# Larger GpSimd shares in the last rows and fewer load-to-load waits in a streaming row maximum

## The chip, the cores and the metric

One core of a Trainium2 chip. The time is device microseconds of one execution, the median of several. In the profile's lines DVE is VectorE, ACT ScalarE, POOL GpSimd and SPq the sequencer of SyncE, which issues the loads; L64 is line 64 of the kernel. Times are from the start of the span.

## The reference

```python
x = np.random.randn(8192, 8192).astype(np.float32)
return np.linalg.norm(x, ord=np.inf, axis=1)      # max |x| of each row
```

268 MB are read once and 32 KB written.

## The kernel before

Loads of two rows per partition (128 x 16384 floats, 8.39 MB) go through a ring of three places. VectorE reduces each with absolute maximum. In the last two loads and the pieces of the last row a share is left to ScalarE (absolute value in place) and GpSimd (maximum); a final reduce on VectorE takes the last piece and the partial results together.

```python
HEAD = 2
PAIRS = 30
TILES = (                                # (width, GpSimd's share of it)
    [[(8192, 0)]] * HEAD
    + [[(16384, 0)]] * (PAIRS - 1)
    + [[(16384, 7168)], [(8192, 3328)]]
    + [[(4160, 1760), (2080, 832), (1024, 384), (512, 0), (416, 0)]]
)
RING = 3 * 16384
...
            if final:
                buf = last[:, :w]
            else:
                if at + w > RING:
                    at = 0
                buf = ring[:, at : at + w]
                at += w
            nc.sync.dma_start(out=buf, in_=src[:, off : off + w])
...
            if final:
                pairs_out()
                absmax(res[:, R - 1 :], last)
```

The program's builder derives the waits. A load that takes over a place waits for the reduce that read it and also for the earlier load that filled it.

## Time and profile before

| | before |
|---|---|
| median of the first 6 runs | 628.58 us (628.52 to 628.62) |
| profiled span | 626.8 us |
| load queue busy | 99.1% of the span |
| between two loads | 19.35 us, of which VectorE works 17.22 |
| semaphore instructions at the load's line | 29 |
| start of the last two-row reduce to the end of the final reduce | 20.86 us |

Read the middle and the end apart. In the middle the stream of loads sets the pace. At the end, once the last two-row load has landed, what counts is who is ready last for the final reduce: the last landing, VectorE or GpSimd. The lines are in the prediction. One more, on the load's own line in the kernel before (engine, kind and count; then minimum, median and maximum in ns, and the first and last start in us):

```profile
L153 SPq EVENT_SEMAPHORE  x29: 17/17/27, 22.7 to 564.6; - x29
```

One extra semaphore instruction goes with each load that takes over a place: the wait for the earlier load, which half of the loads are to lose.

### The profile page before, as it was taken

The page shows a single profiled execution, that of the slowest core. Times are in us where ns is not written, and L with a number is a line of the kernel's source. Part 1 is how long each engine was busy: PE and PEld are TensorE (multiplying, and loading weights), DVE is VectorE, ACT ScalarE, POOL GpSimd, SP SyncE. Part 2 cuts the span into 40 slices and gives each one's busy share as a digit, 9 for nine tenths or more (in the row PEclk, how much of TensorE's full clock was granted, in tenths as well). Part 3 has the DMA queues.
Part 4 walks back from the last instruction along what each step waited for, and adds up shares of the span by engine and source line. Part 5 has one row for each costly group of instructions (what it writes and reads, how often), then busy time and mean ns, then how long its engine had stood idle before and what let it go on. Part 6 is the DMA issues. An engine that isn't in the chain of part 4 may idle for free.

```text
span 626.8 us, 218 instructions
## 1 busy us (share of the span) xinstructions
PE 8.7 (1%) x15; PEld 3.2 (1%) x15; DVE 537.5 (86%) x39; ACT 14.3 (2%) x10; POOL 13.3 (2%) x13
## 2 busy tenths in 40 slices
PE   0000000000000000000000000000000000000005
PEld 0000000000000000000000000000000000000002
DVE  1938988889988889888898888988889988889888
ACT  0000000000000000000000000000000000000034
POOL 0000000000000000000000000000000000000007
PEclk9999999999999999999999999999999999999999
DMA  8999999999999999999999999999999999999996
GB/s 368 435 468 402 468 402 468 402 468 402 468 402 468 402 460 410 452 418 448 422 448 422 418 452 402 468 402 468 402 468 402 468 402 468 402 468 402 460 402 278
DMA packets 5525, 268.47 MB, mean 428 GB/s; under 512 B 627, under 2 KB 789, under 8 KB 1045
## 3 DMA queue, kind: packets, MB, share of 16 engines
q1 hardware_dynamic: 5472, 268.44, 99.1%
q10 hardware_dynamic: 53, 0.03, 0.0%
HBM read 268.44 MB, written 0.03 MB: 428 GB/s over the span
## 4 chain that ended last, share of the span: by engine, by line
DMA 70%; DVE 29%; issue 0%; SPq 0%; PE 0%; ACT 0%; DVEq 0%
DMA ring<-in_x_dram 70%; DVE res L64 28%; DVE part L64 1%; DVE last L64 1%; SPq L153 0%; PE ps_ones L189 0%; ACT sb_ones L190 0%; DVEq L64 0%
## 5 line engine op out<-in xcount | busy, mean ns | idle before, releaser
L64 DVE TENSOR_REDUCE res<-ring 128x2 f32<-128x16384 f32 (+1 forms) x32 | 525.4, 16420 | 86.5 <-DMA ring<-in_x_dram 86.5
L82 ACT ACTIVATE ring<-ring 128x7168 f32<-128x7168 f32 (+4 forms) x5 | 12.2, 2449 | 577.0 <-DMA ring<-in_x_dram 577.0
L71 POOL TENSOR_REDUCE part<-ring 128x1 int32<-128x7168 int32 (+1 forms) x2 | 9.1, 4566 | 587.3 <-ACT ring L82 587.2
L108 PE MATMUL ps_warm<-ident 128*128 128x512 f32 (+1 forms) x12 | 8.2, 827 | 614.5 <-DVE part L64 613.2
L64 DVE TENSOR_REDUCE part<-ring 128x1 f32<-128x1024 f32 (+1 forms) x2 | 6.3, 3210 | 0.0
L108 PEld LDWEIGHTS ps_warm<-ident 128*128 128x128 f32 x12 | 2.9, 274 | 618.8 <-issue 615.3
L64 DVE TENSOR_REDUCE last<-ring 128x1 f32<-128x2400 f32 (+3 forms) x4 | 5.3, 1392 | 0.0
L71 POOL TENSOR_REDUCE last<-ring 128x1 int32<-128x1760 int32 (+2 forms) x3 | 3.0, 1017 | 0.4 <-ACT ring L82 0.4
L96 ACT ACT_TABLE_LOAD x1 | 1.3, 1283 | 31.5 <-DVE res L64 31.5
L64 DVE TENSOR_REDUCE res<-last 128x1 f32<-128x423 f32 x1 | 0.6, 594 | 0.1
L88 POOL MEMSET ident<- 128x128 f32 x1 | 0.2, 205 | 21.4 <-DVE res L64 21.4
L128 ACT COPY sb_pairs<-ps_pairs 30x128 f32<-30x128 f32 x2 | 0.4, 254 | 0.0
L71 POOL TENSOR_REDUCE res<-part 128x1 int32<-128x2 int32 x2 | 0.4, 196 | 0.1
L123 PE MATMUL ps_pairs<-ident,res 128*30 128x128 f32 x2 | 0.4, 272 | 0.0
L190 ACT COPY sb_ones<-ps_ones 4x128 f32<-4x128 f32 x1 | 0.3, 255 | 2.0 <-PE ps_ones L189 2.0
masks.py:199 POOL TENSOR_SCALAR_AFFINE_SELECT ident<-ident 128x128 f32<-128x128 f32 x1 | 0.3, 294 | 0.1
L189 PE MATMUL ps_ones<-ident,res 128*4 128x128 f32 x1 | 0.3, 272 | 1.3 <-DVE res L64 1.3
L123 PEld LDWEIGHTS ps_pairs<-ident,res 128*30 128x30 f32 x2 | 0.2, 106 | 0.6 <-POOL res L71 0.3
L96 ACT ACTIVATE ident<-ident 128x1 f32<-128x1 f32 x1 | 0.2, 203 | 0.0
L208 POOL MEMSET const-float32-0.0<- 128x1 f32 x1 | 0.1, 99 | 0.2 <-issue 0.2
L208 POOL MEMSET const-bfloat16-1.0<- 128x1 bf16 x1 | 0.1, 102 | 0.0
L208 POOL MEMSET const-uint8-127<- 128x1 uint8 x1 | 0.1, 102 | 0.0
(2 smaller groups left out, 0.2 us busy)
## 6 DMA issues: line engine op xcount, KB each, us to landing
ring<-in_x_dram SPq DMA_DIRECT2D x3, 4096.0 KB, 21.5
ring<-in_x_dram SPq DMA_DIRECT2D x1, 2080.0 KB, 35.7
ring<-in_x_dram SPq DMA_DIRECT2D x1, 1040.0 KB, 37.8
ring<-in_x_dram SPq DMA_DIRECT2D x1, 512.0 KB, 38.5
ring<-in_x_dram SPq DMA_DIRECT2D x30, 40.8
ring<-in_x_dram SPq DMA_DIRECT2D x1, 256.0 KB, 38.7
last<-in_x_dram SPq DMA_DIRECT2D x1, 208.0 KB, 38.7
out_dram<-sb_pairs ACTq DMA_DIRECT2D x1, 30.0 KB, 1.5
```

The source lines that it names most:

```text
L64: return keep(nc.vector.tensor_reduce(out=dst, in_=src, axis=X, op=MAX, apply_absolute_value=True,)).ins
L71: keep(pool.add_instruction(mybir.InstTensorReduce(name=nc.get_next_instruction_name(), ins=[pool.lower_ap(src.bitcast(INT32))], outs=[poo ...
L82: keep(nc.scalar.activation(src, src, mybir.ActivationFunctionType.Abs))
L88: nc.gpsimd.memset(ident, 0.0).ins, after.name,
L96: abs_ident = nc.scalar.activation(ident[:, :1], ident[:, :1], mybir.ActivationFunctionType.Abs)
L108: product = keep(nc.tensor.matmul(ps_warm[:, : w * P], lhsT=ident, rhs=ident.unsqueeze(1).to_broadcast([P, w, P]), start=True, stop=True,) ...
L123: keep(nc.tensor.transpose(ps_pairs[r], both[:, :, r], ident))
L128: keep(nc.scalar.copy(sb[:, :, r], ps_pairs[r]))
L189: nc.tensor.transpose(ps_ones, res[:, X_ONE:], ident)
L190: keep(nc.scalar.copy(sb_ones, ps_ones))
L208: nc = _bacc.Bacc("TRN2", target_bir_lowering=False, num_devices=1)
```

## The change

The intent: take work from VectorE at the end, where it is the last to be ready, and drop waits that a later wait contains.

```diff
-    + [[(16384, 7168)], [(8192, 3328)]]
-    + [[(4160, 1760), (2080, 832), (1024, 384), (512, 0), (416, 0)]]
+    + [[(16384, 7328)], [(8192, 3488)]]
+    + [[(4128, 1824), (2048, 864), (1024, 416), (512, 0), (480, 0)]]
...
-            nc.sync.dma_start(out=buf, in_=src[:, off : off + w])
+            load = nc.sync.dma_start(out=buf, in_=src[:, off : off + w]).ins
+            if not final:
+                if (len(loads) + 4) % 10 < 5:
+                    for a, v, earlier in loads:
+                        if a < at and at - w < a + v:
+                            tc.declare_no_dep(
+                                load, earlier, reason="ordered by the reduces in between",
+                            )
+                loads.append((at - w, w, load))
```

More of the change, by code (lines that the diff above doesn't have):

```diff
@@ L131, in pairs_out @@
         ))
+    loads = []
     at = 0
```

## The prediction

> **What bounds the kernel now.** I read the page from the top. Only two things are busy: VectorE, and the DMA engines.
>
> ```profile
> PE 8.7 (1%) x15; PEld 3.2 (1%) x15; DVE 537.5 (86%) x39; ACT 14.3 (2%) x10; POOL 13.3 (2%) x13
> ...
> DMA  8999999999999999999999999999999999999996
> ...
> q1 hardware_dynamic: 5472, 268.44, 99.1%
> ```
>
> The reader is to see that the load queue fills 99.1% of the span while VectorE, the busiest engine, has 86%. The next view is the chain that ended last, in order of time. It is periodic in the middle and of another kind at the end:
>
> ```profile
> 80.77 0.02 issue
> 80.80 17.23 DVE res L64
> 98.03 0.02 issue
> 98.04 40.78 DMA ring<-in_x_dram
> 138.83 0.02 issue
> ...
> 562.46 40.80 DMA ring<-in_x_dram
> 603.26 0.02 issue
> 603.28 8.69 DVE res L64
> 611.97 6.25 DVE part L64 x2
> 618.22 5.25 DVE last L64 x4
> 623.47 0.04 DVEq L64
> ```
>
> From 80.77 to 138.83 us three loads of two rows land: 58.06 / 3 = 19.35 us each. Each is 128 x 16384 x 4 bytes = 8.39 MB, so 433.5 GB/s. The reduce of such a load takes 17.22 us, so VectorE waits 2.13 us for every load. The chain passes through the reduce only because the ring has three places and load n is issued when the reduce of load n-3 ends. That does not make the reduce the limit: the load issued at 98.04 lands 40.78 us later, which is 2.13 us (rest of the load then moving) + 19.35 (the next) + 19.35 (itself) = 40.8. The queue still holds 21.4 us of work when a new load joins it.
>
> At 603.26 the last two-row load has landed and the character changes. From there VectorE has no gap: 8.69 + 6.25 + 5.25 us. The last timeline lines on VectorE, ScalarE and GpSimd give the race at the end:
>
> ```profile
> 613.04 2.98 ACT L82 ACTIVATE ring<-ring 128x3328 f32<-128x3328 f32 x1 [3.50 <-DMA ring<-in_x_dram]
> ...
> 618.14 5.32 DVE L64 TENSOR_REDUCE last<-ring 128x1 f32<-128x2400 f32 x4
> ...
> 619.71 3.08 POOL L71 TENSOR_REDUCE last<-ring 128x1 int32<-128x1760 int32 x3 [0.38 <-ACT ring L82]
> ...
> 623.55 0.59 DVE L64 TENSOR_REDUCE res<-last 128x1 f32<-128x423 f32 x1
> ```
>
> VectorE reaches 623.46, GpSimd 622.79; the last piece, issued at 584.09 with 38.7 us to landing, is there at 622.79. So the final reduce (623.55) waits for VectorE alone, by 0.67 us over both others. After it come 0.28 us of transpose, 0.26 us of copy and the store, all fixed.
>
> **What the Trainium skill says.** (1) "DMA: Bandwidth & Descriptors", section "Where 436 GB/s comes from", puts the ceiling of 16 ports at 435.2 GB/s. This trace has 433.5 in the middle: agreed, and no more than 0.4% can be gained there. (2) The same page, "Anatomy of one DMA": DMA engines do not wait on semaphores; a wait sits on the issuing sequencer before dispatch. The trace agrees: both waits of a load are SyncE's (29 and 29 times, next fence), and a removed wait can only help by an earlier issue. (3) The same page, "Two DMAs through the same engine are not ordered": the order a kernel has is the completion semaphore. The change keeps that order indirectly: the reduce has waited for the earlier load and the new load waits for that reduce. (4) "VectorE: DVE Perf Modes", "The perf-mode tier table": this reduce has only the 1x mode. At the 0.96 GHz that the page gives, one element a cycle is 1.042 ns; the trace's (17220 - 8686) / 8192 = 1.0417 ns agrees.
>
> **The change, part one: the waits.**
>
> ```profile
> SPq L153 <- DVE res L64: 490.9, 29, 17.2
> SPq L153 <- DMA ring<-in_x_dram: 77.7, 29, 20.1
> ```
>
> Each of the 29 loads that takes over a place has two waits. The first is an extra semaphore instruction at the load's line (x29, median 17 ns), which ends when the earlier load lands; the second ends 17.2 us later, when that load's reduce does. For example, SyncE issues at 78.69, waits 1.8 us for the landing at 80.77, then 17.2 us for the reduce until 98.03. The reduce cannot end before its own load has landed, so the DMA wait is always contained in the VectorE wait. Without it, the VectorE wait becomes about 19.0 us and ends at the same 98.03.
>
> Which loads: counting the ring's loads from 0, the condition picks numbers 6 to 10, 16 to 20 and 26 to 30, all of which take over a place, so 15 of the 29 (the one small piece that it also picks, number 36, has no wait instruction of its own now, as its predecessors have made that wait). I expect 14 semaphore instructions to remain at the load's line. Saved: 15 x 17 ns = 0.26 us of SyncE's time, spent while it waits anyway. On the issue of a load: 0. Even if each issue came 20 ns sooner, it would join a queue with 21.4 us in it. **Sum of part one: 0.00 us.**
>
> **Part two: the shares and the pieces.** VectorE's cost from its rows: 1.0417 ns an element plus a fixed 142 ns (1210 for 1024, 5209 for 4864, 675 for 512 all fit). ScalarE's absolute value: (6176 - 2977) / 3840 = 0.833 ns; GpSimd the same, (6164 - 2968) / 3840 = 0.832 ns.
> VectorE's elements, in order after the untouched 8192: 1024 becomes 864 (16384 - 8192 - 7328), 4864 becomes 4704, then 2400 to 2304, 1248 to 1184, 640 to 608, 512 stays, and the final 416 + 7 to 480 + 7. Before the final that is 160 + 160 + 96 + 64 + 32 = 512 elements fewer: 0.533 us. The final has 64 more: +0.067. If nothing else held it, the end would move by -0.467 us.
>
> Now what holds it. Landings: ScalarE starts on a piece some 0.10 us after it lands (603.36 against 603.26), so the one-row load landed at about 612.94. Today VectorE turns to it at 613.01; with 0.167 us less ahead of it, it would at 612.84, so it waits until about 612.96. Gain so far 0.05 instead of 0.167. After this: -0.217 at the next start (617.92; that piece, 32 elements shorter, lands at about 617.83), -0.317 (620.38; lands about 620.27), -0.384 (621.68; lands about 621.50), -0.417 for the 512 piece (622.36; lands about 622.22). The landing estimates are ScalarE's starts less 0.10, less the shift in the cumulated width (32 to 64 elements) at 19.35 us / 16384 = 1.18 ns. All are met with 0.1 us or so to spare. VectorE ends at 623.46 - 0.417 = 623.04. The last byte of the row is the same byte, so the final piece lands at 622.8 as now.
> GpSimd: its first long reduce starts 0.133 us later (609.74) and takes 6.30; the second, 3.10, starts at about 616.22 and ends at 619.32; after the small combine and ScalarE's 1824 (until 619.65) it runs 1.71 + 0.91 + 0.535 with gaps of 0.05, from 619.72 to about 622.97. That is 0.07 us before VectorE.
> So the final starts at about 623.13, takes 0.594 + 0.067 = 0.66, and ends at 623.79 instead of 624.14. **Sum of part two: -0.35 us. Both parts: 628.57 - 0.35 = 628.2 us**, which is 0.06%.
>
> **The rivals.** (a) GpSimd becomes the bound of the end. It is my nearest calculation, 0.07 us. For it: its chain will carry 13,920 elements instead of 13,472 and passes through ScalarE first. Against: today it has 0.67 us of slack. If each of its hand-overs from ScalarE costs 0.1 us more than I took, the end moves only -0.1 to -0.2: 628.4 us.
> (b) The waits cost the DMA stream something that these views don't show, such as a small gap between loads. For it: 433.5 stays 0.4% below the skill's ceiling, and 30 loads x 19.35 x 0.4% is 2.3 us; someone chose to drop exactly half of the waits. Against: the load is in the queue 21.4 us before its turn. If half of that came back, 627.1 us. I give this one chance in twenty.
> (c) The dropped wait comes back elsewhere: another semaphore wait in its place, for instance for the reuse of a semaphore. As it too would lie within the 17.2 us of the VectorE wait, it makes 628.2 as well, unless it waits for a load still moving: that would delay an issue by up to 19 us, of which the queue's 21.4 us covers all. So again nothing.
> (d) The gain at the end is lost because the last landing moves later: three pieces of the last row are a little smaller and begin at other addresses. The last five pieces land within 622.79 - 612.94 = 9.85 us against 9.68 at the steady rate, so all their overheads together are now 0.17 us. Even double that leaves the landing (622.96) before VectorE's 623.04. No change to the estimate.
>
> **Range and chances.** The executions before lie within 0.1 us (628.52 to 628.62). My uncertainties are rival (a), +0.2, the one-row landing, 0.1 either way, and the stream, which repeats to a few hundredths from load to load. The range is 627.85 to 628.6 us. A move of 2% would need 12.6 us. Nothing in the change can give that: the whole end after 603.26 is 23 us, and the stream is at the ceiling. Slower by 2% would need the queue to run dry, 21 us late on an issue. I put faster at 0.01, same at 0.98, slower at 0.01.
>
> **What would show it.** Right: 19.35 us between reduces in the middle and VectorE still waiting 2.13 us before each; 14 instead of 29 semaphore instructions at the load's line, with the waits for VectorE longer by about 1.8 us in those loads and the issues at the same times; in the end a short VectorE wait (up to 0.15 us) before the 4704 reduce, GpSimd's last reduce ending near 622.97, the final reduce of 487 elements starting near 623.13. Wrong: another period in the middle, or a gap in the queue (rival b); the final reduce starting well after VectorE's last one (rival a, or d if the landing is late). The whole would be wrong if the start of the stream moved, since every later time hangs on it.

## The result, and the profile after

The changed kernel took 628.28 us (628.14 to 628.70, 6 runs), the kernel before 628.58 us beside it. The ratio is 0.9996 with an interval of 0.9983 to 1.0009: the same, by the 2% rule. A ratio here is the mean time of one kernel's fast runs over that of the other's fast runs of the same rounds, so it is not quite the ratio of the medians quoted.

The profile alone would have misled. The profiled execution happened to be the slowest of the six, and its span is 626.9 us, 0.1 *longer* than before. First the end of its chain of waits:

```profile
582.27 31.14 DMA ring<-in_x_dram
613.41 0.03 issue
613.43 5.05 DVE part L64
618.49 5.05 DVE last L64 x4
623.54 0.04 DVEq L64
623.57 0.05 issue
623.62 0.67 DVE res L64
```

The chain before had VectorE work without a gap from 603.28 on. Now it comes off a landing at 613.41: VectorE was ready for the one-row load a little before it was there. The rest of the end is shorter: the last two-row reduce starts at 603.72, the final one ends at 623.62 + 0.66 = 624.28, which is 20.56 us against 20.86. So the end gained 0.30 us. The two others that the final reduce needs are GpSimd's last three reduces and the last piece, which was issued at 584.5:

```profile
620.13 3.04 POOL L71 TENSOR_REDUCE last<-ring 128x1 int32<-128x1824 int32 x3
last<-in_x_dram SPq DMA_DIRECT2D x1, 240.0 KB, 38.6
```

GpSimd was done at 623.17 and the piece landed at 623.1; VectorE was done at 623.5 and is still the last.

What hid it is in the middle, in VectorE's timeline of the same execution (start, duration, and in brackets the idle time before):

```profile
80.71 17.22 DVE L64 TENSOR_REDUCE res<-ring 128x2 f32<-128x16384 f32 x1 [2.13 <-DMA ring<-in_x_dram]
100.36 17.22 DVE L64 TENSOR_REDUCE res<-ring 128x2 f32<-128x16384 f32 x1 [2.43 <-DMA ring<-in_x_dram]
119.90 17.22 DVE L64 TENSOR_REDUCE res<-ring 128x2 f32<-128x16384 f32 x1 [2.32 <-DMA ring<-in_x_dram]
139.25 17.22 DVE L64 TENSOR_REDUCE res<-ring 128x2 f32<-128x16384 f32 x1 [2.14 <-DMA ring<-in_x_dram]
```

Two loads are 19.65 and 19.54 us apart instead of 19.35, another later is 19.41. Together that is 0.30 + 0.19 + 0.06 = 0.55 us lost. The first load landed 0.10 us earlier than before, so all that follows is 0.44 us later, and 0.44 - 0.30 is the longer span. Whether that slip belongs to the dropped waits is a question for the experiments.

Of the waits themselves, SyncE's view and the load's line:

```profile
SPq L155 <- DVE res L64: 518.2, 29, 19.3
SPq L155 <- DMA ring<-in_x_dram: 51.4, 14, 20.0
```

The semaphore instructions at the load's line, as above:

```profile
L155 SPq EVENT_SEMAPHORE  x14: 17/1719/1779, 22.6 to 565.0; - x14
```

Fifteen of the 29 waits for a landing are gone. The waits for VectorE, still 29, took 518.2 us instead of 490.9: 27.3 more, or 1.8 for each of the fifteen. The time saved in one wait came back in the next. The first load without its wait was issued at 78.60, before at 78.69: 0.09 earlier, as the whole stream is there (80.71 and 80.80 in the timelines). So dropping the wait did not move the issue. The median length of the semaphore instructions that stay is 1719 ns instead of 17; in both kernels SyncE waits some 1.8 us for such a landing, and why the instruction is recorded longer here isn't known.

### The profile page after: what moved, and what is told of

It reads as the page before. It is cut to its first block, busy times and chain, and to the rows that moved or that the text cites. A ratio compares the mean times of both kernels' runs of the same rounds, so it can differ in the third digit from the quotient of the medians.

```text
span 626.9 us, 203 instructions
## 1 busy us (share of the span) xinstructions
PE 8.8 (1%) x15; PEld 3.3 (1%) x15; DVE 537.1 (86%) x39; ACT 14.7 (2%) x10; POOL 13.5 (2%) x13
## 4 chain that ended last, share of the span: by engine, by line
DMA 70%; DVE 29%; SPq 0%; issue 0%; PE 0%; ACT 0%; DVEq 0%
DMA ring<-in_x_dram 70%; DVE res L64 28%; DVE part L64 1%; DVE last L64 1%; SPq L155 0%; PE ps_ones L201 0%; ACT sb_ones L202 0%; DVEq L64 0%
## 5 line engine op out<-in xcount | busy, mean ns | idle before, releaser
L82 ACT ACTIVATE ring<-ring 128x7328 f32<-128x7328 f32 (+4 forms) x5 | 12.6, 2523 | 577.0 <-DMA ring<-in_x_dram 577.0
L71 POOL TENSOR_REDUCE part<-ring 128x1 int32<-128x7328 int32 (+1 forms) x2 | 9.4, 4697 | 587.9 <-ACT ring L82 587.9
L64 DVE TENSOR_REDUCE part<-ring 128x1 f32<-128x864 f32 (+1 forms) x2 | 6.1, 3048 | 0.1
L64 DVE TENSOR_REDUCE last<-ring 128x1 f32<-128x2304 f32 (+3 forms) x4 | 5.1, 1342 | 0.0
L71 POOL TENSOR_REDUCE last<-ring 128x1 int32<-128x1824 int32 (+2 forms) x3 | 3.0, 1050 | 0.1
L88 POOL MEMSET ident<- 128x128 f32 x1 | 0.2, 204 | 21.3 <-DVE res L64 21.3
## 6 DMA issues: line engine op xcount, KB each, us to landing
ring<-in_x_dram SPq DMA_DIRECT2D x1, 256.0 KB, 38.5
last<-in_x_dram SPq DMA_DIRECT2D x1, 240.0 KB, 38.6
```

Source lines behind the costliest of these rows:

```text
L64: return keep(nc.vector.tensor_reduce(out=dst, in_=src, axis=X, op=MAX, apply_absolute_value=True,)).ins
L71: keep(pool.add_instruction(mybir.InstTensorReduce(name=nc.get_next_instruction_name(), ins=[pool.lower_ap(src.bitcast(INT32))], outs=[poo ...
L82: keep(nc.scalar.activation(src, src, mybir.ActivationFunctionType.Abs))
L88: nc.gpsimd.memset(ident, 0.0).ins, after.name,
```

## The experiments

My theory: the whole gain is at the end, because VectorE was last to be ready there; the dropped waits give nothing, as each lay within the wait for VectorE. Rivals: the dropped waits speed up the stream; they disturb it; GpSimd or the last landing is what binds the end. Times, and those of the kernel before on the same chip:

| run | what it is | median, us | before, us | end, us |
|---|---|---|---|---|
| e1 | new shares and pieces only | 628.39 | 628.81 | 20.56 |
| e2 | dropped waits only | 628.65 | 628.81 | 20.86 |
| e3 | the change, all waits dropped | 628.57 | 628.81 | 20.56 |
| e4 | the change again | 628.46 | 628.81 | 20.55 |
| e5 | still larger GpSimd shares | 628.87 | 628.77 | 21.06 |
| e6 | last pair as single rows | 628.79 | 628.77 | |
| e7 | ring of two places | 661.24 | 628.77 | |
| e8 | waits dropped in runs of fifteen, one run | 628.39 | 628.77 | 20.56 |
| e9 | single rows, fewer pieces | 628.69 | 628.56 | |
| e10 | the change a third time | 628.26 | 628.56 | 20.57 |

The last column is the yardstick: from the start of the last two-row reduce to the end of the final reduce. It is left out for e7 and where the end is built otherwise. e1 to e4 shared one set of runs of the kernel before (9). For e5 to e8 the record lists the same nine values and one more, so their "before" was mostly taken some minutes earlier; those runs are judged by their traces. e9 and e10 have a set of their own (9), on another chip. All results were correct.

### The two halves of the change alone (e1, e2)

e1 is the kernel before with the new `TILES`; e2 is the changed kernel with the old ones.

```diff
# e2, against the changed kernel
-    + [[(16384, 7328)], [(8192, 3488)]]
-    + [[(4128, 1824), (2048, 864), (1024, 416), (512, 0), (480, 0)]]
+    + [[(16384, 7168)], [(8192, 3328)]]
+    + [[(4160, 1760), (2080, 832), (1024, 384), (512, 0), (416, 0)]]
```

> Only the new shares and pieces, with all waits of the kernel before. Theory (the end is bound by VectorE, the waits do nothing): the whole gain, 628.25 us, 0.3 us under the kernel before, and the end relative to the start of the last two-row reduce as in the changed kernel (final reduce ends 20.57 us after it). Rival (the dropped waits give the gain): 628.55. Scatter of the executions: under 0.15 us if the dropped waits cause the scatter of the changed kernel (628.14 to 628.70), up to 0.5 us if it is chance.

> Only the dropped waits, with the shares and pieces of before. Theory: 628.57 us within 0.05, the loads 19.35 us apart, the final reduce ends 20.86 us after the start of the last two-row reduce, 14 semaphore instructions at the load. Rival (the waits cost the stream something): 628.3 or less, with loads closer than 19.35. Second rival (dropping them disturbs the stream): a median above 628.65 and a scatter of 0.5 us.

e1 took 628.39 us, 0.42 less than the kernel before beside it; e2 took 628.65, 0.16 less, with the kernel before scattering from 628.55 to 629.10. Taken alone, those times leave a little room for the rival. The end of e2's VectorE timeline decides more:

```profile
603.21 8.69 DVE L64 TENSOR_REDUCE res<-ring 128x1 f32<-128x8192 f32 x1 [2.14 <-DMA ring<-in_x_dram]
...
623.48 0.59 DVE L64 TENSOR_REDUCE res<-last 128x1 f32<-128x423 f32 x1
```

and of e1's:

```profile
603.54 8.69 DVE L64 TENSOR_REDUCE res<-ring 128x1 f32<-128x8192 f32 x1 [2.14 <-DMA ring<-in_x_dram]
...
623.44 0.66 DVE L64 TENSOR_REDUCE res<-last 128x1 f32<-128x487 f32 x1
```

The end is 20.86 us with the old pieces and 20.56 with the new, whatever the waits: e2 has the figure of the kernel before, e1 that of the changed one. In between, e2's two-row reduces start 19.34 to 19.36 us apart all along, as before. What is left of the 0.16 us is no more than the scatter, and e3 doesn't repeat it.

e1 also has a slip, with all its waits in place: two of its reduces start at 100.28 and 119.78, 19.50 us apart. So a slip needs no dropped wait.

### All waits dropped (e3), and in other runs (e8)

```diff
-                if (len(loads) + 4) % 10 < 5:
+                if True:                                # e3
+                if (len(loads) + 4) % 20 < 15:          # e8
```

> The changed kernel with the wait for the earlier load dropped from all loads instead of half. Theory: as the changed kernel, 628.25 us within 0.1; no semaphore instruction left at the load. If dropped waits help the stream, another 0.1 us or more under it; if they disturb it, twice the scatter and a higher median.

e3 took 628.57 us, 0.11 *more* than e4 with half of the waits dropped, which is within the scatter. If dropped waits helped, it should be the other way round. And one expectation was plainly wrong. The load's line in e3:

```profile
L155 SPq EVENT_SEMAPHORE  x25: 17/17/17, 98.3 to 562.8; - x25
```

Not 0 but 25 semaphore instructions are there: another wait took the place of the one removed. The page attributes all of SyncE's waiting at the loads to VectorE, none to a load, so these wait for something that has long happened. My reading: the loads use eight semaphores in turn, and before one is used again SyncE must know that its last load has landed. The first half can be checked: the kept traces name the semaphore that each load signals (the views do not print it), and in e3, e8 and the kernels before and after there are eight, in turn. Loads 8 to 32 are 25. In the change five loads without the wait follow five with it. Load n needs news of load n - 8. Each load that keeps its wait waits for the load three before it, so load n - 5 has brought that news. Then nothing comes back, which would explain why half of the waits were dropped and not all. e8 tests this reading by its count:

> Waits dropped in runs of fifteen loads instead of five. With all of them dropped 25 short semaphore instructions stood at the load again, the first ahead of load 8: I take it that the loads use eight semaphores in turn, and one is waited for before it is used again unless a later wait has told of it. Then this one has 7 waits of its own left and 13 to 15 come back (loads 8 to 10 and 21 to 30, perhaps two more), 20 to 22 in all. If nothing comes back: 7. The time is the same either way, 628.4.

```profile
L155 SPq EVENT_SEMAPHORE  x20: 17/17/1760, 98.5 to 564.7; - x20
```

20 it is: seven of its own and thirteen that came back. The time is 628.39 us in one run, the end 20.56 us. Rival (c) of the prediction, a wait that returns for the reuse of a semaphore, is real, though not in this change, and as harmless as it said.

### The change again (e4, e10)

> The changed kernel once more, to see whether the profiled slip of its stream (two loads 19.65 and 19.54 us apart instead of 19.35) comes at the same loads again. Theory (chance): 628.25 us, another profile without a slip or with one elsewhere. Rival (it belongs to the loads with dropped waits): the same two loads late by 0.3 and 0.2 us again, and a scatter of 0.5 us.

> The changed kernel beside it on the same chip, as the measure for a difference of 0.2 us, and a third profile of its stream. Theory: 628.45 us, loads 19.35 us apart with a slip at most by chance, the final reduce ends 20.57 us after the start of the last two-row reduce.

628.46 and 628.26 us, 0.35 and 0.30 below the kernel before beside them, after 0.30 in the first comparison. e10's two-row reduces start 19.34 to 19.36 us apart from first to last. e4 had one of 0.10 us at another load: 158.25 to 177.70 is 19.45. The slip is not at the same loads again, so nothing ties it to the loads without waits, and e1 has one without any dropped wait. All slips of 0.05 us or more in the kept traces (the changed kernel, e1, e3, e4 and e8) lie between 80 and 178 us; the other runs with three places have none. Whether they are more frequent with dropped waits was not tested: only the kernel before and e1 were profiled with all waits. What makes them isn't known.

### More for GpSimd (e5)

```diff
-    + [[(16384, 7328)], [(8192, 3488)]]
-    + [[(4128, 1824), (2048, 864), (1024, 416), (512, 0), (480, 0)]]
+    + [[(16384, 7648)], [(8192, 3808)]]
+    + [[(4128, 1984), (2048, 944), (1024, 464), (512, 0), (480, 0)]]
```

> The changed kernel with GpSimd's shares larger once more (7648, 3808, 1984, 944, 464). By my model of the end (landings, 1.0417 ns an element on VectorE, 0.833 on ScalarE and GpSimd) VectorE is ready 20.6 us after the last landing of two rows less 1.1, so 19.47, GpSimd at 20.17, and the final reduce ends at 20.97 instead of 20.57: GpSimd has become the bound, 628.7 us. Rival (VectorE was still the bound and GpSimd has room): 0.3 us faster than the changed kernel. Rival (the last landing is the bound): no change.

628.87 us; the end is 21.06 us long, 0.50 more than with the change (20.97 was forecast). VectorE's timeline in e5:

```profile
613.12 4.72 DVE L64 TENSOR_REDUCE part<-ring 128x1 f32<-128x4384 f32 x1 [0.40 <-DMA ring<-in_x_dram]
618.02 4.97 DVE L64 TENSOR_REDUCE last<-ring 128x1 f32<-128x2144 f32 x4 [0.18 <-DMA ring<-in_x_dram]
623.80 0.66 DVE L64 TENSOR_REDUCE res<-last 128x1 f32<-128x487 f32 x1 [0.81 <-POOL last L71]
```

VectorE now waits three times: for two landings, since it has too little to do, and 0.81 us for GpSimd. The bound has changed hands, so the change's shares lie between too little and too much. That the last landing was not the bound in the changed kernel is not shown by e5 but by that kernel's own trace (623.1 against VectorE's 623.5).

### A ring of two places (e7)

All of the above says that the moment of issue is harmless. This run asks when it stops being so.

```diff
-RING = 3 * 16384
+RING = 2 * 16384
```

> The changed kernel with a ring of two places instead of three: each load is issued some 2.1 us before the load then moving lands, with nothing else in the queue. Theory (the moment of issue matters only when the queue runs dry): the first load needs 11.9 us from issue to landing for 9.7 us of data, so 2.2 us are not data; with 2.1 us left in the queue each load is 0.1 to 0.5 us late, 19.5 to 19.9 us apart, 631 to 643 us in all. Rival (the moment of issue never matters here): 628.3, 19.35 us apart.

661.24 us (656.48 to 664.93): the direction of the theory, but a far larger loss than it said. VectorE's timeline in e7:

```profile
102.30 17.22 DVE L64 TENSOR_REDUCE res<-ring 128x2 f32<-128x16384 f32 x1 [2.48 <-DMA ring<-in_x_dram]
123.93 17.22 DVE L64 TENSOR_REDUCE res<-ring 128x2 f32<-128x16384 f32 x1 [4.41 <-DMA ring<-in_x_dram]
143.49 17.22 DVE L64 TENSOR_REDUCE res<-ring 128x2 f32<-128x16384 f32 x1 [2.35 <-DMA ring<-in_x_dram]
165.28 17.22 DVE L64 TENSOR_REDUCE res<-ring 128x2 f32<-128x16384 f32 x1 [4.56 <-DMA ring<-in_x_dram]
```

In a ring of two, the idle time before a reduce is also the lead with which the next load was issued ahead of the landing then awaited. A lead of 2.48 us gives a next start 21.63 us later, 4.41 gives 19.56, 2.35 gives 21.79. All loads with a lead of 4 us or more came within 19.94 us; those with less than 3 came either within 19.7 or between 21.2 and 23.3. In this one trace the two kinds part almost cleanly: all ten leads of 2.35 us or less were followed by more than 21.2 us, and seven of the eight from 2.41 to 2.72 by less than 19.6 (2.48 is the exception). Why so little in the lead should cost two to four microseconds stays open. With three places the lead is 21.4 us, and nothing of this shows.

### A build meant to beat both (e6, e9)

If VectorE could begin on the last rows sooner, the last landing would be the bound, and the final reduce could be short. Both load the last pair as two single rows.

```diff
# e6 (and partial results of a row in several columns)
-PAIRS = 30
+PAIRS = 29
...
+    + [[(16384, 0)]] * PAIRS
+    + [[(8192, 3520)], [(8192, 5056)], [(5632, 2400), (2560, 1696)]]
+    + [[(3488, 1120), (1760, 832), (1120, 640), (736, 352), (448, 192), (320, 0), (320, 0)]]
# e9: HEAD = 0, PAIRS = 30
+    + [[(16384, 0)]] * PAIRS
+    + [[(8192, 4096)], [(8192, 5312)], [(8192, 3552)]]
+    + [[(3904, 1984), (2048, 832), (1152, 512), (576, 0), (512, 0)]]
```

> The last pair loaded as two single rows, so that VectorE can start 9.7 us earlier on it, larger shares for GpSimd and a final piece of 320 elements: built to beat both. By the model VectorE and GpSimd are both ready 0.07 us before the last landing, which becomes the bound, and the final reduce ends at 623.39 instead of 623.83 on the clock of the kernel before: 0.45 us faster than the changed kernel. Rival (single rows cost the stream time): the landings of the last rows later by more than 0.1 us, and no gain.

> The build with single last rows missed because it had ten small loads at the end: its last piece landed at 623.1 instead of 622.8 and the one before it only at 622.74. This one has eight, the smallest 512 elements, keeps four rows in the last transpose (the two single rows at the head become a pair) and gives VectorE and GpSimd 0.06 us of room at the last landing. If the number of small loads was the cause, the last landing is back at 622.8 and the final reduce ends at 623.6, 0.2 us before the changed kernel's 623.85 (on the clock of the kernel before): 628.25 us beside the changed kernel's 628.45. If not, no gain again.

Both missed: 628.79 and 628.69 us, no better than the kernel before; e9 is 0.43 us behind e10, which ran beside it. VectorE did start earlier, and the end did become a matter of landings, but of later ones. The chain of e9:

```profile
582.76 37.55 DMA ring<-in_x_dram
620.30 0.02 issue
620.33 1.42 DVE last L64
621.75 0.02 issue
621.77 1.51 DVE last L64 x2
623.28 0.04 DVEq L64
623.31 0.05 issue
623.36 0.71 DVE res L64
```

VectorE waits for the 2048-element piece until 620.30. The next piece, of 1152, was issued at 583.2 and took 38.5 us, so it landed at 621.7, just as VectorE was done with the one before (621.75). The model had it land at 621.3 (583.90, where the last two-row load without a share for GpSimd lands in the kernel before, plus 31,680 elements at 19.35 us for 16,384), or 621.4 as this run's stream is 0.08 us later. The last piece was issued at 584.2 and took 38.9 us, so it was there at 623.1 instead of 622.8. In e6 it was 610.0 + 13.1 = 623.1 too. Fewer pieces did not mend it, so their number was not the whole cause; what delays these landings is not settled. No build tried here beats the changed kernel.

## Why the prediction was right

The prediction was 628.2 us within 627.85 to 628.6; the first comparison gave 628.28. That the absolute figure is so near is partly luck: the median of the kernel before alone is 628.58, 628.81 and 628.56 in its three sets. What the prediction has to answer for is the difference at the end.

- **The two bounds.** Right: the stream in the middle and VectorE at the end. e1 shows the latter: with less work for VectorE, more for GpSimd and the same last byte, the end is 0.30 us shorter. e5 hands the bound to GpSimd.
- **Part one, 0.00 us.** Right, with its count (14 left) and the waits for VectorE longer by 1.8 us each. e2's end and spacing are those of the kernel before, and e3 is no faster than e4. The issue of the first load without its wait did not move.
- **Part two, -0.35 us.** The yardstick shows -0.30. The final reduce was to start at 623.13 on the clock of the kernel before; it started at 623.62 - 0.44 = 623.18. Most of the 0.05 us is an estimated landing: the one-row load was put at 612.94, ScalarE's start less 0.10 us, and VectorE was to go on at 612.96. The landing was at 613.41 - 0.44 = 612.97, and VectorE went on at 613.43 - 0.44 = 612.99.
- **Rival (a), GpSimd.** Nearer in the forecast than in fact. GpSimd was to end at 622.97, 0.07 us before VectorE. It ended at 620.13 + 3.04 - 0.44 = 622.73, which is 0.35 us before VectorE (623.52 - 0.44 = 623.08). The term that was off is the gap: 0.05 us were added between its last three reduces, whose durations come to 3.15 us (3 x 1.050), yet they took 3.04 together; they overlap a little.
- **Rival (b), something in the stream.** It fell as it was put: with the waits dropped the loads stay 19.35 us apart. The prediction did not foresee that single loads slip by 0.1 to 0.3 us in some executions. The changed kernel's six runs scatter by 0.56 us where those of before scatter by 0.10, and one lay outside the range for that reason; in the set beside e1 to e4 the kernel before scattered by 0.55 as well.
- **Rivals (c) and (d).** (c) appeared in e3 and e8 and cost nothing. For (d), the last landing in the changed kernel is 584.5 + 38.6 - 0.44 = 622.7: not later.

## What to carry to other kernels

Before removing a wait, look at what its engine waits for next: a wait contained in a longer one was worth nothing here, and its time moved into the next wait. In a stream-bound kernel, tune the end by comparing the last landing and every engine's last work, and measure it from a common event near the end, because a stumble of the stream elsewhere can be larger than the gain. One profiled execution is not the median one.

## What the Trainium skill lacked or had wrong

- "DMA: Bandwidth & Descriptors", section "Where 436 GB/s comes from", says without a condition that for HBM to SBUF the HBM side, about 358 GB/s, binds. On this one core the loads ran at 433.5 GB/s (8.39 MB every 19.35 us) in all the builds with three places. The condition is on the same page, in the note to its measured table: that its figures, up to 425 GB/s, are those of one core with the other of the pair idle, and that about 358 is what each gets when both stream. The section named lacks it.
- "GPSIMD Engine Reference", section "Engine selection", sends a reduction along the free dimension to VectorE and names no case for GpSimd. Here GpSimd's integer maximum took 0.832 ns an element, less than VectorE's 1.042, though it needs ScalarE's absolute value first (0.833 ns).
- No page I found says how far ahead a load must be issued to keep the queue full. In e7 leads of 2.1 to 2.35 us left loads 21.3 to 23.2 us apart, those of 2.41 to 2.72 all but one within 19.6, and 4 us or more all within 19.94.
- None tells of the slips of single loads: 0.06 to 0.30 us at a time, up to 0.55 us in one execution, with and without dropped waits, all between 80 and 178 us of the span.
